# Gate and up of the last token block as seven products of halves, with the sums of weights formed one block earlier

## Chip, core and metric

One core of one Trainium2 chip runs the whole kernel. The metric is the device time of one execution in microseconds (us). The core has five engines, each of which works through its own list of instructions in order: TensorE (PE; its weight loads are shown apart as PEld), VectorE (DVE), ScalarE (ACT), GpSimd (POOL) and SyncE (SP), which issues nearly all transfers. The transfers themselves run on 16 DMA engines.

## The reference

One layer of a sequence model with 2048 tokens, D = 1024, everything in float32. Four mixers (S5, HGRN2, FoX attention, mLSTM) work on projections of the normed input; their outputs are joined, projected by `w_out`, and a gated feed-forward follows, each with a norm before and after:

```python
        mix = jnp.concatenate([y_a, y_b, y_c, y_d], axis=-1) @ w_out[l]
        h = h + rms_norm(mix, ln_mix_post[l])
        a = rms_norm(h, ln_ffn_pre[l])
        ff = (jax.nn.silu(a @ w_ffn_gate[l]) * (a @ w_ffn_up[l])) @ w_ffn_down[l]
        h = h + rms_norm(ff, ln_ffn_post[l])
```

The change concerns `a @ w_ffn_gate` and `a @ w_ffn_up`; both weights are 1024 x 2816.

## The kernel before, in words

**Numbers.** TensorE multiplies in a format (fp32r) that holds only the upper part of a float32. So each operand is split into two such parts, hi and lo, and each product is three matmuls: hi by hi, lo by hi, hi by lo. In the names, a weight's parts are wh and wl (dh and dl for the down weights), an activation's b_ah and b_al.

**Blocks.** The 2048 tokens are worked in four blocks of 512 (b = 0 to 3), a block being four row tiles of 128. The mixers of block b + 1 are laid beside the feed-forward of block b; the last block's feed-forward has nothing beside it. For each block `Attn.proj` first multiplies by `w_out`, and then, for each row tile t, takes a square sum, forms 1/rms on GpSimd (L1415, L1416), loads the row of x (b_xt, L1419), adds it, stores the sum for later (h_d, L1421), takes a second norm (rsqrt_mean, L67 and L68 on GpSimd), and hands the normed row to `transpose_parts`: eight 128 x 128 transposes on TensorE (L102), in two groups of four, each of which is copied as hi by ACT (L104) and subtracted as lo by DVE (L105). b_xt has two buffers (pool `x`).

**Feed-forward.** The 2816 columns are 22 tiles f of 128. For each f, `gate_up` loads the gate and up weights (four tiles of 128 x 1024, 512 KB each) and runs 48 matmuls (L1469): gate and up, times eight pieces of D, times three parts, each with 512 token columns. The first two f run in two cuts of 256 columns, so that the first cut needs only row tiles 0 and 1. Then tanh (ACT, L1473), two DVE operations, a hi copy and a lo subtraction give g_h. For two f at a time `down` multiplies by the down weights (eight loads of 256 KB; 48 matmuls, L1494) and adds into b_acc on DVE (L1499).

**Weights.** `split_load` reads a weight in the first block into a raw tile (wr), forms hi on ACT (L87) and lo on GpSimd (L88), and stores both parts to DRAM; from the second block on it reloads the two parts with two SP loads (L83). The rings wh, wl, dh and dl have four buffers each, wr has two. A load waits on SP until its buffer's last reader is done, and what is behind it in SP's list waits too.

**Order.** The program's text names the work, and a scheduler that ran when the kernel was built put it in an order on each engine. The engines then run that fixed order.

The functions that the change touches, and what calls them:

## Time and profile before

| | before |
|---|---|
| median of 3 runs | 2805.01 us (2796.91 to 2816.34) |
| the profiled execution, its own time | 2805.62 us |
| its span on the core | 2803.9 us |
| PE, matmuls | 2692.5 us, 96% of the span |
| PEld, weight loads | 2270.0 us, 81% |
| DVE | 1541.4 us, 55% |
| POOL | 837.9 us, 30% |
| ACT | 778.3 us, 28% |
| moved by DMA | 605.04 MB, mean 216 GB/s |

The busy time of an engine is the time in which at least one of its instructions is running. PE's matmuls overlap each other, so its busy time is no sum of single durations, and the price of one more matmul is read from start to start. PEclk is the share of full TensorE clock granted in a stretch; a DMA share of 1 means that all 16 DMA engines were moving all the time. The gap of 1.7 us between span and time lies outside of the traced instructions.

### The profile page before, as it was taken

How to read it: one execution, taken by the hardware profiler on the slowest of the kernel's cores; microseconds unless marked ns; L12 is line 12 of the kernel's file. 1: busy time of each engine (PE TensorE's matmuls, PEld its weight loads, DVE VectorE, ACT ScalarE, POOL GpSimd, SP SyncE). 2: the span in 40 equal slices, each digit the busy share in tenths (PEclk: the TensorE clock that was granted, in tenths of full speed). 3: DMA queues.
4: the chain of work that ended last, by engine and by line, in shares of the span. 5: the costliest groups of instructions: out<-in, count | busy, mean ns of one | idle time of the engine just before them, and what ended most of it. 6: DMA issues, size and time to landing. Idle time of an engine off the chain costs nothing.

```text
span 2803.9 us, 39055 instructions
## 1 busy us (share of the span) xinstructions
PE 2692.5 (96%) x14294; PEld 2270.0 (81%) x14294; DVE 1541.4 (55%) x2522; ACT 778.3 (28%) x1502; POOL 837.9 (30%) x927
## 2 busy tenths in 40 slices
PE   6898999999999999999899999999999999999998
PEld 5787987988888778787787788888878788888886
DVE  7958466483225665865466656545666554322333
ACT  5322336233223333324221232222122331200001
POOL 7554311243125567542111234211022330100001
PEclk9899999999999999999999999999999999999999
DMA  6573696535778878696756566575656656755553
GB/s 228 195 261 123 207 293 209 169 122 210 241 230 292 287 258 282 201 310 232 255 172 214 198 195 206 177 285 187 215 181 194 202 182 230 285 195 186 193 195 135
DMA packets 323103, 605.04 MB, mean 216 GB/s; under 512 B 56160, under 2 KB 146144, under 8 KB 322656
## 3 DMA queue, kind: packets, MB, share of 16 engines
q1 hardware_dynamic: 321888, 602.48, 64.2%
q8 instruction: 113, 1.85, 0.3%
q14 instruction: 78, 0.64, 0.1%
q0 software_dynamic: 1024, 0.07, 0.0%
HBM read 428.42 MB, written 173.35 MB: 215 GB/s over the span
## 4 chain that ended last, share of the span: by engine, by line
PE 73%; DVE 9%; DMA 8%; issue 3%; POOL 2%; SPq 2%; ACT 2%; POOLq 0%; DVEq 0%; ACTq 0%
PE pf L1469 29%; PE pf L1494 15%; PE pf L1386 6%; PE pf L288 5%; PE pf L270 5%; PE ps L903 2%; DVE hQ L511 2%; PE ps L887 1%; PE ps L886 1%; PE ps L828 1%; DVE hA L525 1%; DMA b_xt<-in_x_dram 1%; PE pt L102 1%; PE ps L521 1%; DMA wh<-wu1h 1%
## 5 line engine op out<-in xcount | busy, mean ns | idle before, releaser
L1469 PE MATMUL pf<-b_ah,wh 128*128 128x512 f32 (+1 forms) x1536 | 580.5, 378 | 4.4 <-ACT b_ah L104 4.4
L1469 PE MATMUL pf<-b_ah,wl 128*128 128x512 f32 (+1 forms) x1536 | 579.8, 378 | 0.0
L1469 PE MATMUL pf<-b_al,wh 128*128 128x512 f32 (+1 forms) x1536 | 578.2, 378 | 0.0
L1494 PE MATMUL pf<-dh,g_h 128*128 128x512 f32 x1408 | 461.3, 396 | 1.8 <-DVE b_acc L1499 1.5
L1469 PEld LDWEIGHTS pf<-b_ah,wh 128*128 128x128 f32 x1536 | 291.3, 190 | 60.4 <-ACT b_ah L104 5.3
L1469 PEld LDWEIGHTS pf<-b_ah,wl 128*128 128x128 f32 x1536 | 291.3, 190 | 55.0
L1469 PEld LDWEIGHTS pf<-b_al,wh 128*128 128x128 f32 x1536 | 289.5, 189 | 54.4
L1494 PEld LDWEIGHTS pf<-dh,g_h 128*128 128x128 f32 x1408 | 264.8, 189 | 58.7 <-DVE b_acc L1499 3.4
L1494 PE MATMUL pf<-dl,g_h 128*128 128x512 f32 x704 | 277.5, 394 | 0.0
L1499 DVE TENSOR_TENSOR b_acc<-b_acc,pf 128x512 f32<-128x512 f32 x320 | 215.7, 684 | 105.9 <-PE pf L1494 103.5
L900 POOL TENSOR_TENSOR f_accs<-f_accs,f_pe 128x512 f32<-128x512 f32 (+3 forms) x144 | 172.7, 1199 | 293.6 <-ACT f_pe L894 290.7
L88 POOL TENSOR_TENSOR wl<-wr,wh 128x1024 fp32r<-128x1024 f32 (+2 forms) x76 | 185.6, 2444 | 208.6 <-ACT wh L87 137.3
L896 DVE TENSOR_TENSOR f_pl<-f_pe,f_ph 128x512 fp32r<-128x512 f32 (+3 forms) x160 | 184.6, 1162 | 88.9 <-ACT f_ph L895 75.7
L288 PE MATMUL pf<-wl,aTh 128*128 128x256 f32 (+2 forms) x768 | 220.7, 287 | 0.2 <-DMA wl<-wi_1l 0.2
L288 PE MATMUL pf<-wh,aTh 128*128 128x256 f32 (+2 forms) x768 | 220.7, 288 | 0.0
L288 PE MATMUL pf<-wh,aTl 128*128 128x256 f32 (+2 forms) x768 | 220.2, 287 | 0.0
L1473 ACT ACTIVATE g_th<-pf 128x512 f32<-128x512 f32 x88 | 52.5, 597 | 412.2 <-PE pf L1469 412.1
L1474 DVE SCALAR_TENSOR_TENSOR g_th<-g_th,pf 128x512 f32<-128x512 f32 x88 | 60.3, 685 | 191.8 <-ACT g_th L1473 191.5
L270 PE MATMUL pf<-aTh,wh 128*128 128x512 f32 (+1 forms) x400 | 158.9, 398 | 2.7 <-ACT aTh L104 2.7
L270 PE MATMUL pf<-aTh,wl 128*128 128x512 f32 (+1 forms) x400 | 157.7, 395 | 0.0
L270 PE MATMUL pf<-aTl,wh 128*128 128x512 f32 (+1 forms) x400 | 156.9, 394 | 0.1
L1475 DVE TENSOR_TENSOR g_th<-g_th,pf 128x512 f32<-128x512 f32 x88 | 60.2, 684 | 174.8 <-PE pf L1469 174.7
(510 smaller groups left out, 4812.7 us busy)
## 6 DMA issues: line engine op xcount, KB each, us to landing
dh<-wd_0h SPq DMA_DIRECT2D x66, 256.0 KB
dl<-wd_0l SPq DMA_DIRECT2D x66, 256.0 KB
dh<-wd_1h SPq DMA_DIRECT2D x66, 256.0 KB
dl<-wd_1l SPq DMA_DIRECT2D x66, 256.0 KB
wr<-in_w_ffn_gate_dram SPq DMA_DIRECT2D x22, 512.0 KB
wr<-in_w_ffn_up_dram SPq DMA_DIRECT2D x22, 512.0 KB
dr<-in_w_ffn_down_dram SPq DMA_DIRECT2D x44, 256.0 KB
f_KB<-kb_d SPq DMA_DIRECT2D x80, 132.0 KB
```

The lines of the kernel that those rows point to most:

```text
L88: nc.gpsimd.tensor_tensor(lo, r, f32(hi), ALU.subtract)
L270: nc.tensor.matmul(l3(pt)[:, cut], lhsT=x[k][:, s], rhs=a[:, cut, k], start=(n == 0), stop=(n == 23))
L288: nc.tensor.matmul(pt[:, :w], lhsT=a[:, t, k], rhs=x[k], start=(n == 0), stop=(n == 23))
L511: nc.vector.tensor_tensor(Q[s, hh].rearrange("p (n w) -> p n w", w=h), q3[s, :, h - 1:2 * h - 1], eq[s], ALU.mult)
L896: nc.vector.tensor_tensor(pl[:, cs], pe[:, cs], f32(ph[:, cs]), ALU.subtract)
L900: nc.gpsimd.tensor_tensor(accs[:, cs], accs[:, cs], pe[:, cs], ALU.add)
L1386: nc.tensor.matmul(pt, lhsT=a[:, t, k], rhs=w, start=(first and i == 0), stop=(last and i == 2))
L1469: nc.tensor.matmul(l3(pt)[:, s], lhsT=x[:, k], rhs=a[:, s, k], start=(k == 0 and i == 0), stop=(k == KD - 1 and i == 2))
L1474: nc.vector.scalar_tensor_tensor(th, th, 1.0, pts[0], ALU.add, ALU.mult)
L1475: nc.vector.tensor_tensor(th, th, pts[1], ALU.mult)
L1494: nc.tensor.matmul(pt, lhsT=a[:, s], rhs=w[:, 0], start=(m == 0), stop=(m == 3 * len(fs) - 1))
L1499: nc.vector.tensor_tensor(acc[:, t, ns], acc[:, t, ns], pt, ALU.add)
```

## The change

In the **last block** gate and up are no longer 22 times two products of 512 tokens with D = 1024. Two tiles f and f + 1 form a pair q (11 pairs), and for a pair the tokens are halved (row tiles 0, 1 and row tiles 2, 3), D is halved, and the columns are halved (f and f + 1). The eight products of halves become seven (the scheme of Strassen in Winograd's form), between sums of halves. Each of the seven is 24 matmuls of 256 columns: gate and up, four pieces of D, three parts.

- Activations: `Halves.put` forms the sums of rows T1 to T4 and transposes seven operands of 256 tokens and 512 of D into g_U, 56 transposes in all where there were 32. b_xt of row tiles 2 and 3 takes a buffer of wr.
- Weights: products 0, 2 and 5 use the stored hi and lo parts as they are, in four loads of 256 KB each. Products 1, 3, 4 and 6 use sums of weights: one load of 512 KB in full float32, then hi on ACT and lo on DVE (1 and 4) or GpSimd (3 and 6).
- Results: partial sums lie in a tile C, and DVE makes seven adds of 512 columns for each pair out of PSUM.
- Order: products 0 and 2 of the first two pairs come first (`head`); they need row tiles 0 and 1 alone.

In the **third block** (b = 2) `Halves.keep` forms the sums of weights: for each pair, for gate and for up, SP loads four quarters (256 KB each, in pieces of 512 B), GpSimd makes four sums in place, and GpSimd's own queue stores them to DRAM. The four tiles (ws_0 to ws_3) have one buffer each. This makes 22 groups of four loads, four sums and four stores.

The diff, cut to its core:

```diff
-    for h in range(0, KD, 4):
+    for h in range(0, x.shape[1] // P, 4):
...
+class Halves:
+    def __init__(self, c):
+        self.c = c
+        self.w = [x[0].rearrange("(k p) n -> p k n", p=P) for x in (c.w_ffn_gate, c.w_ffn_up)]
+        self.kept = {(q, i): c.dram.tile([P, D], F32, name=f"ws{q}_{i}") for q in range(c.w_ffn_gate.shape[2] // (2 * P))
+                     for i in (1, 3, 4, 6)}
+    def keep(self, pool, q, m):
+        nc = self.c.nc
+        tiles = [pool.tile([P, 512], F32, name=f"ws_{n}", tag=f"ws_{n}") for n in range(4)]
+        for r, k, f in zip(tiles, (0, 0, 4, 4), (0, 1, 1, 0)):
+            n0 = (2 * q + f) * P
+            nc.sync.dma_start(r.rearrange("p (k n) -> p k n", k=4), self.w[m][:, k:k + 4, n0:n0 + P])
+        X11, X21, X22, X12 = tiles
+        for i, s, x, y, op in ((3, X11, X11, X21, ALU.subtract), (4, X21, X21, X22, ALU.add),
+                               (1, X22, X22, X11, ALU.subtract), (6, X12, X12, X22, ALU.subtract)):
+            nc.gpsimd.tensor_tensor(s, x, y, op)
+        for i, s in ((3, X11), (4, X21), (1, X22), (6, X12)):
+            nc.gpsimd.dma_start(self.kept[q, i][:, m * 512:m * 512 + 512], s)
+    def load(self, q, i):
+        c, nc = self.c, self.c.nc
+        hi, lo = (c.pw.tile([P, WRING], F32R, name=n, tag=n)[:, 0:D] for n in ("wh", "wl"))
+        if i in (0, 2, 5):
+            k0, f = {0: (0, 0), 2: (512, 0), 5: (512, 1)}[i]
+            for t, part in ((hi, 0), (lo, 1)):
+                for m, n in enumerate("gu"):
+                    nc.sync.dma_start(f32(t[:, m * 512:m * 512 + 512]),
+                                      c.parts[f"w{n}{2 * q + f}"][part][:, k0:k0 + 512])
+            return hi, lo
+        nc.sync.dma_start(f32(lo), self.kept[q, i])
+        nc.scalar.activation(hi, f32(lo), AF.Copy)
+        (nc.vector if i in (1, 4) else nc.gpsimd).tensor_tensor(lo, f32(lo), f32(hi), ALU.subtract)
+        return hi, lo
+    def operand(self, i, t):
+        u = self.U[:, 2 * i + t].rearrange("p (d k t) -> p d k t", d=2, k=4)
+        return u[:, 0], u[:, 1]
+    def put(self, t, xs, rows):
+        c, nc = self.c, self.c.nc
+        a, b = slice(0, 512), slice(512, D)
+        if t < 2:
+            new = ((0, xs[t][:, a]), (2, xs[t][:, b]))
+        else:
+            x, x1 = xs[t - 2], xs[t]
+            s1, s2 = rows(), rows()
+            T1, T2, T3, T4 = s1[:, a], s1[:, b], s2[:, a], s2[:, b]
+            nc.vector.tensor_tensor(T1, x1[:, a], x[:, a], ALU.subtract)
+            nc.vector.tensor_tensor(T2, x1[:, b], T1, ALU.subtract)
+            nc.gpsimd.tensor_tensor(T3, x1[:, b], x1[:, a], ALU.subtract)
+            nc.vector.tensor_tensor(T4, x[:, b], T2, ALU.subtract)
+            new = ((1, T2), (3, T3), (4, T1), (5, T4), (6, x1[:, b]))
+        for i, v in new:
+            transpose_parts(c, c.psS, "s", v, *self.operand(i, t % 2))
...
-    def proj(self, b):
+    def proj(self, b, halves=None):
...
-            xt = self.xtile("b_xt")
+            if halves is None or t < 2:
+                xt = self.xtile("b_xt")
+            else:
+                xt = c.pwr.tile([P, WRING], F32, name="b_xt2", tag="wr")[:, 0:D]
...
-            transpose_parts(c, c.psS, "s", xt, ah[:, t], al[:, t])
+            if halves is None:
+                transpose_parts(c, c.psS, "s", xt, ah[:, t], al[:, t])
+            else:
+                xs.append(xt)
+                halves.put(t, xs, self.row)
...
-    def run(b, hook):
+    def run(b, hook, step, halves):
...
+        def gate_up_halves():
+            C = attn.p.tile([P, 4, D], F32, name="g_c", tag="b_al").rearrange("p t n -> p (t n)")
+            C = C.rearrange("p (b q j m t) -> p b q j m t", b=2, q=2, j=2, m=2)
+            def product(q, i):
+                wh, wl = halves.load(q, i)
+                pt = ptile()
+                pv = pt.rearrange("p (m j t) -> p m j t", m=2, j=2)
+                for m in range(2):
+                    for k in range(4):
+                        for n, (w, d) in enumerate(((wh, 0), (wl, 0), (wh, 1))):
+                            k0 = (4 * m + k) * P
+                            nc.tensor.matmul(pv[:, m], lhsT=w[:, k0:k0 + P],
+                                             rhs=halves.U[:, 2 * i:2 * i + 2, d * 512 + k * P:d * 512 + (k + 1) * P],
+                                             start=(k == n == 0), stop=(k == 3 and n == 2))
+                return pt.rearrange("p (m t) -> p m t", m=2)
+            def add(dst, pt, x):
+                nc.vector.tensor_tensor(dst, pt, x, ALU.add)
+            def gated(f, v):
+                th, h = p2.tile([P, BLK], F32, name="g_th", tag="th"), h_tile()
+                t, h4 = (x.rearrange("p (j t) -> p j t", t=256) for x in (th, h))
+                nc.scalar.activation(t, v[:, :, 0], AF.Tanh, scale=0.5)
+                nc.vector.scalar_tensor_tensor(t, t, 1.0, v[:, :, 0], ALU.add, ALU.mult)
+                nc.vector.tensor_tensor(t, t, v[:, :, 1], ALU.mult)
+                nc.scalar.activation(h4[:, 0:2], t, AF.Copy, scale=0.5)
+                nc.vector.scalar_tensor_tensor(h4[:, 2:4], t, 0.5, f32(h4[:, 0:2]), ALU.mult, ALU.subtract)
+                pend.append((f, h[:, 0:BLK], h[:, BLK:]))
+            def head(q):
+                c1 = C[:, q % 2, 0]
+                nc.scalar.activation(c1[:, 1], product(q, 0), AF.Copy)
+                add(c1[:, 0], product(q, 2), c1[:, 1])
+            def tail(q):
+                c1, c2 = C[:, q % 2, 0], C[:, q % 2, 1]
+                add(c1[:, 1], product(q, 1), c1[:, 1])
+                add(c2[:, 0], product(q, 3), c1[:, 1])
+                pt = product(q, 4)
+                add(c1[:, 1], pt, c1[:, 1])
+                add(c2[:, 1], pt, c2[:, 0])
+                add(c1[:, 1], product(q, 6), c1[:, 1])
+                gated(2 * q, c1)
+                add(c2[:, 0], product(q, 5), c2[:, 0])
+                gated(2 * q + 1, c2)
+            for q in range(NF // 2):
+                if q == 0:
+                    head(0)
+                    head(1)
+                elif q > 1:
+                    head(q)
+                tail(q)
+                if q:
+                    down(pend[:2], q == 1)
+                    del pend[:2]
...
-        gate_up((0, 1), (slice(0, 2), slice(2, 4)))
-        for f in range(2, NF):
+        if halves is not None:
+            gate_up_halves()
+        else:
+            gate_up((0, 1), (slice(0, 2), slice(2, 4)))
+        for f in range(2, NF if halves is None else 0):
+            if f % 2 == 0:
+                step(f // 2 - 1)
             gate_up((f,), (slice(0, 4),))
             if len(pend) == 3 and f < NF - 1:
                 down(pend[:2], pend[0][0] == 0)
                 pend = pend[2:]
+        step(NF // 2 - 1)
...
+        halves = Halves(c)
+        sums = None
+
+        def step(b, q):
+            if b == NB - 2:
+                for m in range(2):
+                    halves.keep(sums, q, m)
+
         for b in range(NB):
+            last = b == NB - 1
+            if last:
+                stack.close()
+                pool = s.enter_context(tc.tile_pool(name="g_u", bufs=1, side="left", reuse_waits="tile"))
+                halves.U = pool.tile([P, 14, D], F32R, name="g_U")
             if b:
-                attn.proj(b)
+                attn.proj(b, halves if last else None)
+            if b == NB - 2:
+                stack = ExitStack()
+                sums = stack.enter_context(tc.tile_pool(name="w_sums", bufs=1, side="left", reuse_waits="tile"))
             if b + 1 < NB:
                 mixers(b + 1)
-            ffn(b, lambda: attn.pre(b + 1) if b + 1 < NB else None)
+            ffn(b, lambda: attn.pre(b + 1) if b + 1 < NB else None, lambda q: step(b, q), halves if last else None)
```

**Where the instructions stand.** First SP's list at the start of the third block's feed-forward. b_xt is the row of x, h_d the stored row, wg1h the hi part of the gate weights of tile 1, ws_ a tile of the sums. Before:

```order
L1419 DMA b_xt<-in_x_dram 128x1024
L1421 DMA h_d_224<-b_acc 128x1024 x2
L1419 DMA b_xt<-in_x_dram 128x1024
L83 DMA wh<-wg1h 128x1024
L83 DMA wl<-wg1l 128x1024
L83 DMA wh<-wu1h 128x1024
L83 DMA wl<-wu1l 128x1024
L83 DMA dh<-wd_0h 128x512
```

and in the changed kernel:

```order
L1490 DMA b_xt<-in_x_dram 128x1024 x2
L1354 DMA ws_20926<-in_w_ffn_gate_dram 128x4x128
L1354 DMA ws_20927<-in_w_ffn_gate_dram 128x4x128
L1354 DMA ws_20928<-in_w_ffn_gate_dram 128x4x128
L1354 DMA ws_20929<-in_w_ffn_gate_dram 128x4x128
L1492 DMA h_d_224<-b_acc 128x1024 x2
L83 DMA wh<-wg1h 128x1024
L83 DMA wl<-wg1l 128x1024
L83 DMA wh<-wu1h 128x1024
L83 DMA wl<-wu1l 128x1024
L83 DMA dh<-wd_0h 128x512
```

A whole group of four sum loads now stands between the loads of b_xt and the stores of the rows, ahead of the weights of tile 1.

Second, GpSimd's list at the same place, where it forms the 1/rms of the row tiles (L1415, L1416, L67 and L68 before; L1483, L1484, L67 and L68 after). Before:

```order
L1404 TENSOR_SCALAR b_ss<-b_ss 128x4
L1415 TENSOR_SCALAR b_rs<-b_ss 128x1
L1416 TENSOR_TENSOR b_rs<-b_rs,mhalf 128x1
L67 TENSOR_SCALAR b_rs<-b_rs 128x1
L68 TENSOR_TENSOR b_rs<-b_rs,mhalf 128x1
L1415 TENSOR_SCALAR b_rs<-b_ss 128x1
```

and in the changed kernel, in the second row tile:

```order
L1484 TENSOR_TENSOR b_rs<-b_rs,mhalf 128x1
L1358 TENSOR_TENSOR ws_20926<-ws_20926,ws_20927 128x512
L1358 TENSOR_TENSOR ws_20927<-ws_20927,ws_20928 128x512
L1360 DMA ws_3_8752<-ws_20926 128x512
L1358 TENSOR_TENSOR ws_20928<-ws_20928,ws_20926 128x512
L1360 DMA ws_4_8753<-ws_20927 128x512
L67 TENSOR_SCALAR b_rs<-b_rs 128x1
L1483 TENSOR_SCALAR b_rs<-b_ss 128x1
L1358 TENSOR_TENSOR ws_20929<-ws_20929,ws_20928 128x512
L1360 DMA ws_1_8751<-ws_20928 128x512
L68 TENSOR_TENSOR b_rs<-b_rs,mhalf 128x1
```

The sums and their stores now stand between the steps of one row tile's 1/rms.

Third, SP's list in the middle of the last block. ws_1_8763 is a stored sum (product 1 of a pair), wg11h a stored hi part. Before:

```order
L83 DMA dl<-wd_0l 128x512
L83 DMA dh<-wd_0h 128x512 x2
L83 DMA dl<-wd_0l 128x512
L83 DMA dl<-wd_1l 128x512
L83 DMA dh<-wd_1h 128x512 x2
L83 DMA dl<-wd_1l 128x512
L83 DMA wl<-wg17l 128x1024
L83 DMA wh<-wg17h 128x1024
```

and in the changed kernel:

```order
L1373 DMA wl<-ws_1_8763 128x1024
L1373 DMA wl<-ws_3_8764 128x1024
L83 DMA dl<-wd_0l 128x512
L83 DMA dh<-wd_0h 128x512 x2
L83 DMA dl<-wd_0l 128x512
L83 DMA dl<-wd_1l 128x512
L83 DMA dh<-wd_1h 128x512 x2
L83 DMA dl<-wd_1l 128x512
L1373 DMA wl<-ws_4_8765 128x1024
L1373 DMA wl<-ws_6_8766 128x1024
L1370 DMA wl<-wg11l 128x512
L1370 DMA wh<-wg11h 128x512
```

The down weights stand where they stood, between groups of gate and up loads; the loads of products 1 and 3 stand ahead of them and those of 4, 6 and 5 behind.

## Rows read from the trace of the kernel before

**Rows 1.** The page's first part: engine, busy us, share, instructions.

```profile
PE 2692.5 (96%) x14294; PEld 2270.0 (81%) x14294; DVE 1541.4 (55%) x2522; ACT 778.3 (28%) x1502; POOL 837.9 (30%) x927
```

**Rows 2.** Stretches: us; busy PE, PEld, DVE, ACT, POOL (instructions); PEclk, DMA share, GB/s.

```profile
1800.00:2200.00 400.00, 395.89 (x1923) 323.91 (x1922) 222.68 (x338) 94.65 (x187) 75.41 (x92) 1.00 0.65 217
...
1900.00:1910.00 10.00, 8.71 (x65) 7.96 (x64) 4.39 (x5) 3.21 (x8) 2.60 (x4) 1.00 1.01 375
...
2441.00:2780.00 339.00, 339.00 (x1504) 277.56 (x1504) 98.28 (x144) 26.45 (x43) 0.00 (x0) 1.00 0.56 186
```

**Rows 3.** PE's waits, 2400 to 2804: who for whom, sum us, times, longest.

```profile
PE pf L1469 <- ACT b_ah L104: 1.7, 2, 1.4
PE pt L102 <- DVE b_xt L1425: 1.4, 1, 1.4
```

**Rows 4.** The chain in order of time: start us, us, what.

```profile
269.03 20.14 PE pf L288 x169
...
1905.58 9.06 DMA b_xt<-in_x_dram
...
2422.73 7.89 DMA b_xt<-in_x_dram
```

**Rows 5.** Stretches, line L1469 alone: PE busy, PEld busy, PEclk, DMA share, GB/s.

```profile
2437.00:2448.00 11.00, 11.00 (x97) 11.00 (x98) 1.00 0.55 187
...
2422.00:2434.00 12.00, 11.37 (x96) 11.19 (x96) 1.00 1.02 378
...
2448.00:2780.00 332.00, 224.61 (x962) 180.21 (x960) 1.00 0.55 184
```

**Rows 6.** Timeline of PE at the last block's start: us, us of one, what, count.

```profile
2426.13 1.03 PE L102 MATMUL pt<-ident,b_xt 128*128 128x128 f32 x8
2426.92 0.37 PE L1469 MATMUL pf<-b_al,wh 128*128 128x256 f32 x1
```

**Rows 7.** Groups by line and shape: count; busy us, mean ns; idle before, releasers.

```profile
L88 POOL TENSOR_TENSOR wl<-wr,wh 128x1024 fp32r<-128x1024 f32 x72 | 174.9, 2430 | 201.6 <-ACT wh L87 130.3 <-DMA ka_d<-flo 53.8 <-DMA dr<-in_w_ffn_down_dram 8.0
...
L900 POOL TENSOR_TENSOR f_accs<-f_accs,f_pe 128x512 f32<-128x512 f32 x96 | 134.3, 1399 | 213.4 <-ACT f_pe L894 211.7
...
L87 ACT ACTIVATE wh<-wr 128x1024 fp32r<-128x1024 f32 x72 | 76.0, 1055 | 85.2 <-PE pf L1469 24.8 <-DMA wr<-in_w_ffn_gate_dram 19.1 <-PE pf L270 12.0
...
L105 DVE TENSOR_TENSOR b_al<-pt,b_ah 128x512 fp32r<-128x512 f32 x64 | 41.6, 685 | 44.2 <-ACT b_ah L104 43.9
...
L1530 DVE TENSOR_TENSOR b_acc<-b_acc,g_h 128x1024 f32<-128x1024 f32 x12 | 14.8, 1229 | 7.6 <-DMA g_h<-in_ln_ffn_post_dram 4.8 <-ACT junk L1332 2.6
```

**Rows 8.** Timeline of SP in the last block: us, us, DMA issue.

```profile
2575.11 0.32 SPq L83 DMA_DIRECT2D wl<-wg11l  x1
2575.53 0.38 SPq L83 DMA_DIRECT2D wh<-wg11h  x1
```

**Rows 9.** DMA traffic from 2570 to 2580 in 40 slices of 0.25 us.

```profile
GB/s 41 180 377 393 418 401 328 279 295 262 319 377 221 139 90 16 0 0 0 0 0 0 0 0 131 147 147 262 262 377 311 426 377 442 426 377 377 131 0 0
```

**Rows 10.** Timeline of SP around and in the third block's feed-forward.

```profile
1800.66 0.56 SPq L83 DMA_DIRECT2D dl<-wd_1l  x1
...
2056.68 0.33 SPq L83 DMA_DIRECT2D wl<-wg9l  x1
...
2102.80 0.32 SPq L83 DMA_DIRECT2D wl<-wg11l  x1
...
2190.21 0.32 SPq L83 DMA_DIRECT2D wl<-wg15l  x1
```

**Rows 11.** GpSimd's own transfers: ns of an issue (min, median, max), when; landing.

```profile
L872 POOL DMA_DIRECT2D f_QB<-f_mr x32: 497/520/814, 461.5 to 2192.8; - x32
...
DMA to landing us min/median/max: 1.6/3.5/5.6
```

1 line of the change is left out of this document (added).

## The prediction

> **What bounds the kernel now.** I read the page first, then the stretches of the two blocks that the change touches, then what TensorE waits for there, then the chain. The page's first part says that TensorE has a matmul in flight for 96% of the span [rows 1]. The stretches say it more sharply: over the last block's feed-forward (2441 to 2780 us) PE is busy in all 339 us, at full clock (PEclk 1.00, which is the 2.4 GHz level), with DVE at 98, ACT at 26 and GpSimd at 0 us, and the DMA engines at a share of 0.56 [rows 2]. PE waits there for nothing but 1.7 and 1.4 us at the block's start [rows 3]. So a matmul column taken away in this block is time taken away, as long as nothing new makes PE wait. In the third block (1800 to 2200 us) PE is busy for 395.9 of 400 us, the DMA engines have a share of 0.65 and move 217 GB/s, and GpSimd works 75 us; but in its start, 1900 to 1910, the DMA share is already 1.01 at 375 GB/s and PE is idle for 1.3 of 10 us [rows 2]. There the chain runs through a transfer: the load of b_xt takes 9.06 us of it, as the like load in the last block takes 7.89 [rows 4]. So the last block has room on every engine but PE, and the third block has room on GpSimd, little on the DMA engines, and none at its start.
>
> **The products (last block).** Before: 22 tiles f, of which two run in two cuts of 256 columns (192 matmuls) and 20 run as 48 matmuls of 512 (960). After: 11 pairs times 7 products times 24 matmuls of 256 columns = 1848. PE's matmuls overlap, so their price is from start to start. 962 of 512 columns take 224.61 us: 0.2335 each. 97 of 256 columns take 11.00 us: 0.1134 each with a DMA share of 0.55; 96 take 11.37 us, 0.1184 each, with a share of 1.02 [rows 5]. The longest unbroken run of 256-column matmuls, of another line, is 169 in 20.14 us, 0.1192 each [rows 4]. Halving the columns costs almost nothing, then: the 128-column weight load before each stays hidden. The new block moves, for each pair, 5 MiB of gate and up weights (three products of 1 MiB, four of 0.5) and 2 MiB of down weights, where 6 MiB moved before; a pair takes about 30 us, so 7.34 MB in 30.3 us is 242 GB/s, against 186 now, a DMA share of 0.56 x 242/186 = 0.73. Between the two prices at 0.55 and 1.02 that gives 0.1153. Before: 960 x 0.2335 + 192 x 0.1134 = 245.9 us. After: 1848 x 0.1153 = 213.1. **Saved: 32.8 us**; bounds 36.3 (at 0.1134) and 25.7 (at 0.1192).
>
> The Trainium skill (TensorE: Matmul & The Clock Gate, section "Wait — 56ns, not 53.3ns?") has start-to-start at the columns divided by 2.4 GHz plus about 2.5 ns, which is 109.2 ns for 256 columns and 215.8 ns for 512. By that page's figures the saving would be an estimated 228.1 - 201.8 = 26.3 us, not 32.8. The trace does not agree: its 512-column matmuls of this line cost 0.2335, more than two of 256 (0.1134 each), so the rows decide.
>
> **The operands.** The 32 transposes of the block become 56. Eight take 0.79 us from start to start [rows 6], so 24 more are 2.4 us of PE: **+2.4 us**. Each four of them need an ACT copy and a DVE subtraction of 0.69 us [rows 7], and the last two row tiles need three more DVE operations and one on GpSimd. They are covered by the four products (0 and 2 of the first two pairs, 96 matmuls, 11 us) that need only the first two row tiles. Those tiles' b_xt no longer wait for a buffer of two, so they can start earlier than the 7.89 us transfer lets them now; the 3.1 us of waiting may go or may grow by as much. Taken as 0; ends -3 and +5.
>
> **The ring of four (last block).** A product's weights go into a ring of four, so a load starts when the product four before it ends and must be ready three products, 3 x 24 x 0.1153 = 8.3 us, later. Two loads of 512 KB issued at 2575.1 and 2575.5 [rows 8] move their bytes between 2576.0 and 2579.5 (40 slices of 0.25 us) [rows 9]: 4.4 us for 1 MB, an estimated 3.5 for one. Then the ACT copy (1.06) and the subtraction, 1.23 on DVE (products 1 and 4) or 2.43 on GpSimd (3 and 6) [rows 7]: 3.5 + 1.06 + 2.43 = 7.0 us. It fits with 1.3 us to spare, and for half of the products 11 us of down matmuls lie between as well. DVE's work for a pair, 7 adds, 6 gating operations, 8 down adds and 2 subtractions, is 21 x 0.69 + 2.5 = 17 us of 30. I take **+2 us**; ends 0 and 13 (below).
>
> **The sums (third block).** 22 groups of four 256 KB loads by SP, four GpSimd sums and four stores by GpSimd's own queue: 23.1 MB read and 23.1 MB written. In SP's order the first load stands behind a down weight load that SP issued at 1800.66, and the last before the load of gate tile 15, issued at 2190.21 [rows 10]. That is 389.6 us, 17.7 us for a group and 118 GB/s on top of 217, 335 in all; the full stretch moved 375. So on average they fit, with a duty near 0.9. GpSimd's part is 88 sums of 1.40 [rows 7] and 88 issues, for which the nearest row is 0.52 us for a small DMA [rows 11]: 169 us on top of the 75 it does in 400. It has the time.
>
> At the block's start they do not fit. Around the b_xt loads SP now issues a group (1 MB), with about as many stores in flight, where the share was 1.01: 2.1 MB at 375 GB/s are 5.6 us by which b_xt, and the weights of tile 1, come later, on the chain. GpSimd puts two sums and their stores between the two halves of a row tile's 1/rms as well (the order rows). **+6 us**; ends 0 (the groups' loads wait themselves) and 12.
>
> The Trainium skill (DMA: Bandwidth & Descriptors, section "Issuing engines are not separate DMA queues") says that a queue of another engine runs on the same 16 DMA engines and saves issue time alone. It speaks against expecting anything of GpSimd's own queue; this trace agrees only so far that the share reaches 1.01 with nearly all bytes on one queue, and nothing in it shows two queues with much to move. Had the stores engines of their own, the start would cost 2.8 us, not 5.6.
>
> In the rest of the block SP's weight loads run well ahead: tile 9's are issued at 2056.68, and its buffer is freed, for tile 11's, at 2102.80 [rows 10]; its gate product takes 24 x 0.2335 = 5.6 us, so it begins near 2097. That is 40 us ahead, 36 after a landing of 4.4. This hides the slips of single groups. **+2 us**; ends 0 and 54 (below).
>
> **Sum:** -32.8 + 2.4 + 0 + 2 + 6 + 2 = -20.4 us. The profiled execution took 2805.62 us, 0.6 over the median of the three runs: 2785.2, forecast **2785 us**.
>
> **The rivals.** *Everything added is hidden*: the products and transposes alone, -30.4, up to -33.9 with the lowest price: 2772 to 2775. For it: the bursts of [rows 9] leave the DMA engines idle between; against it: 1.01 at the third block's start.
>
> *The ring is too short.* If a landing in the last block takes 6 us, as loads on the chain do where much is queued (7.89 and 9.06 for this size [rows 4]), product 6 is ready after 9.5 us, 1.2 late in each of 11 pairs: +13 instead of +2, 2796 us; at 7 us it is +24, 2807. For it: the eight down loads stand right ahead of product 4's in SP's order. Against it: the DMA share is 0.73 there.
>
> *Slower: SP stands still before a slot.* The four tiles of a group have one buffer each. A load of the next group waits on SP until the store from its tile has landed, and behind it wait all weight loads. Chain of a slot: landing, two sums, two issues, landing: 4.4 + 2.8 + 1.0 + 4.4 = 12.6 us, under the 17.7 that SP's order gives it. With both landings at the 9.06 us of the full stretch [rows 4] it is 21.9: each of 22 groups slips 4.2 us, 92 in all, less the 36 that the ring hides: +56 instead of +2, **2839 us**. It costs nothing below a period of 17.7 + 36/22 = 19.3 us, and eats the gain at 20.3. For it: 335 GB/s on average for 390 us. Against it: the bursts reach 375 and more, and 9 us is a landing at full share.
>
> **How the numbers follow.** Forecast (2777 to 2796) 0.53; all hidden (2772 to 2777) 0.20; ring (2796 to 2807) 0.12; SP (2800 to 2840) 0.15, of which 0.09 above 2833. Measurement of this kernel can tell about 1%, 28 us: faster by over that is below 2777, so 0.20; slower above 2833, so 0.09; within, 0.71. The range 2772 to 2812 leaves out 0.05 below and some 0.13 above.
>
> **What would show it.** The last block's line of products should have 1848 matmuls at 0.113 to 0.119 us start to start, and 2441 to the end some 30 us shorter. A ring that is too short shows as PE waiting for ACT or GpSimd on wh or wl, once per pair. The third block's start should show PE's wait for b_xt grown by some 6 us, and a DMA share near 0.9 until about 2190. The slower rival shows as SP waiting for GpSimd's stores for more than 4 us per group and PE waiting for DMA on weights. I am wrong if PE's idle time in the third block grows by over 20 us, or if the products cost above 0.125 us.

## The result and the profile after

The changed kernel takes 2824.27 us (median of 7 runs, 2818.59 to 2832.87), the kernel before 2805.01 (7 runs). The ratio is 1.0072, with a 95% interval of 1.0051 to 1.0094: 19 us slower, where 20 us faster was forecast, and outside the range of 2772 to 2812.

The profiled execution has a span of 2831.1 us, 27.2 over before's. Below it is cut at the first matmul of a block's `w_out` product (stages) and at PE's last matmul (end):

| us | up to third block | third block | last block | end | span |
|---|---|---|---|---|---|
| before | 1857.4 | 517.0 | 417.0 | 12.5 | 2803.9 |
| after | 1866.3 | 542.3 | 405.3 | 17.2 | 2831.1 |
| difference | +8.9 | +25.3 | -11.7 | +4.7 | +27.2 |

The first column is scatter: in kernels that differ only from the third block on it lies between 1848.8 and 1866.3. Without it 18.3 us are left, near the 19.3 between the medians. So the last block gained two fifths of what was forecast (11.7 of 28.4 us), the third block lost three times as much (25.3 for 8), and the end, which the sum did not have, lost too.

The page's first part after, which answers [rows 1]:

```profile
PE 2684.2 (95%) x15014; PEld 2295.6 (81%) x15014; DVE 1666.4 (59%) x2633; ACT 835.0 (29%) x1563; POOL 1064.5 (38%) x1127
```

Stretches after, with the columns of [rows 2]: two at the third block's start, one in its middle, two in the last block:

```profile
1866.00:1906.00 40.00, 35.38 (x142) 28.30 (x141) 17.39 (x15) 5.75 (x14) 20.94 (x24) 0.91 1.00 358
1906.00:1946.00 40.00, 31.06 (x189) 27.51 (x188) 18.32 (x19) 11.13 (x22) 23.66 (x31) 0.89 0.84 295
2006.00:2186.00 180.00, 174.42 (x769) 138.84 (x768) 110.92 (x160) 32.82 (x61) 99.77 (x108) 0.99 0.94 307
2450.00:2500.00 50.00, 46.67 (x349) 44.13 (x349) 36.08 (x44) 21.69 (x33) 17.39 (x14) 0.97 0.82 284
2600.00:2800.00 200.00, 199.91 (x1375) 186.14 (x1375) 113.65 (x152) 45.97 (x58) 29.69 (x12) 1.00 0.68 223
```

The same first two stretches of the kernel before:

```profile
1857.00:1897.00 40.00, 40.00 (x175) 32.57 (x174) 18.45 (x20) 8.73 (x20) 7.23 (x14) 1.00 0.79 297
1897.00:1937.00 40.00, 35.98 (x269) 33.02 (x268) 22.73 (x33) 13.27 (x28) 9.63 (x17) 0.96 0.65 237
```

In the first 80 us of the third block the DMA share is 1.00 and 0.84 where it was 0.79 and 0.65, PE runs 331 matmuls instead of 444, and its granted clock is 0.91 and 0.89. This is a mean: most of the time it is at 2.4 GHz, but at 1.2 GHz from 1892.5 to 1899.3, 1923.2 to 1926.7 and 1940.3 to 1947.1, stretches that begin in or right behind the three gaps of PE there. In the whole third block 20.5 us are at 1.2 GHz, where it was 3.4. In the middle the share is 0.94 and PE is idle 5.6 us of 180. In the last block PE has no gap over 0.3 us from 2551 to 2802; between 2600 and 2800 it is busy 199.91 of 200 us.

What PE waited for longest from 1790 to the end (sum us, times, longest), which answers [rows 3]; and what SP waited for longest from 1780 to 2420 (SPq is SP's list):

```profile
PE pt L102 <- DVE b_xt L1496: 8.7, 2, 6.6
PE ps L828 <- DMA f_KB<-kb_d: 4.8, 3, 2.5
PE pf L1453 <- ACT junk L1332: 4.6, 1, 4.6
```

```profile
SPq L1354 <- DMA ws<-ws: 117.2, 48, 7.1
```

The first and third of PE's waits lie at the block's start, the second in its middle: f_KB is a load for FoX attention, which runs beside the feed-forward. SP stood 117 us before tiles of the sums whose store had not landed. One such case: SP stands from 2120.7 to 2127.4, the f_KB loads behind it in its list are issued at 2132.1 and 2135.3, and PE stands for f_KB from 2137.5 to 2140.0. The loads of the sums (ns of an issue, then first and last start), and the landing of their stores:

```profile
L1354 SPq DMA_DIRECT2D ws<-in_w_ffn_gate_dram x44: 367/384/2875, 1809.5 to 2201.6; - x44
L1354 SPq DMA_DIRECT2D ws<-in_w_ffn_up_dram x44: 368/384/459, 1832.8 to 2217.8; - x44
```

```profile
DMA to landing us min/median/max: 2.4/5.2/7.3
```

22 groups from 1809.5 to 2217.8, 408.3 us, are 18.6 us each.

### The profile page after: what moved, and what is told of

Its sections match the earlier page's. It is cut to its first block, busy times and chain, and to the rows that moved or that the text cites. A ratio compares the mean times of both kernels' runs of the same rounds, so it can differ in the third digit from the quotient of the medians.

```text
span 2831.1 us, 41412 instructions
## 1 busy us (share of the span) xinstructions
PE 2684.2 (95%) x15014; PEld 2295.6 (81%) x15014; DVE 1666.4 (59%) x2633; ACT 835.0 (29%) x1563; POOL 1064.5 (38%) x1127
## 5 line engine op out<-in xcount | busy, mean ns | idle before, releaser
L1544 PE MATMUL pf<-b_ah,wh 128*128 128x512 f32 (+1 forms) x1152 | 438.4, 381 | 1.7 <-ACT b_ah L104 1.7
L1544 PE MATMUL pf<-b_ah,wl 128*128 128x512 f32 (+1 forms) x1152 | 437.8, 380 | 0.0
L1544 PE MATMUL pf<-b_al,wh 128*128 128x512 f32 (+1 forms) x1152 | 434.9, 379 | 0.0
L1544 PEld LDWEIGHTS pf<-b_ah,wh 128*128 128x128 f32 x1152 | 219.8, 191 | 43.1 <-ACT b_ah L104 2.2
L1544 PEld LDWEIGHTS pf<-b_ah,wl 128*128 128x128 f32 x1152 | 219.8, 191 | 41.1
L1544 PEld LDWEIGHTS pf<-b_al,wh 128*128 128x128 f32 x1152 | 218.1, 190 | 40.8
L1569 PE MATMUL pf<-g_U,wh 128*128 128x256 f32 x1232 | 224.5, 284 | 2.2 <-ACT wh L1374 1.1
L1569 PEld LDWEIGHTS pf<-g_U,wh 128*128 128x128 f32 x1232 | 191.9, 191 | 3.6 <-ACT wh L1374 1.5
L1569 PE MATMUL pf<-g_U,wl 128*128 128x256 f32 x616 | 173.0, 284 | 1.0 <-POOL wl L1375 0.9
L1358 POOL TENSOR_TENSOR ws<-ws,ws 128x512 f32<-128x512 f32 x88 | 119.0, 1352 | 137.3 <-DMA ws<-in_w_ffn_up_dram 60.3
```

The source lines that it names most:

```text
L1358: nc.gpsimd.tensor_tensor(s, x, y, op)
L1544: nc.tensor.matmul(l3(pt)[:, s], lhsT=x[:, k], rhs=a[:, s, k], start=(k == 0 and i == 0), stop=(k == KD - 1 and i == 2))
L1569: nc.tensor.matmul(pv[:, m], lhsT=w[:, k0:k0 + P], rhs=halves.U[:, 2 * i:2 * i + 2, d * 512 + k * P:d * 512 + (k + 1) * P], start=(k == n ...
```

## Experiments

Ratios are to runs of the kernel before on the same chip and use all runs, so they are not the quotient of the two medians; the last three columns are lengths in the profiled execution, as in the table above. e14 and e15 have one run each.

| run | median us (before) | ratio, 95% | third block | last block | end |
|---|---|---|---|---|---|
| e1, no sums | 2792.9 (2804.5) | 0.9949, 0.9931 to 0.9968 | 517.4 | 402.5 | 11.4 |
| e2, sums only | 2830.7 (2804.5) | 1.0093, 1.0069 to 1.0116 | 540.3 | 416.8 | 18.0 |
| e3, loads only | 2816.8 (2804.5) | 1.0041, 1.0028 to 1.0054 | 531.1 | 417.8 | 12.1 |
| e4, stores by SP | 2823.2 (2804.5) | 1.0066, 1.0045 to 1.0088 | 550.3 | 406.0 | 11.4 |
| e5, held back | 2820.1 (2804.0) | 1.0054, 1.0037 to 1.0071 | 541.7 | 405.4 | 17.2 |
| e6, no stores | 2825.1 (2804.0) | 1.0069, 1.0049 to 1.0088 | 541.2 | 416.9 | 12.2 |
| e7, cuts of 256 | 2804.6 (2804.0) | 0.9999, 0.9984 to 1.0013 | 517.3 | 413.9 | 12.5 |
| e8, two blocks | 2854.3 (2804.0) | 1.0170, 1.0154 to 1.0185 | 517.6 | 404.8 | 17.3 |
| e9, two blocks, held | 2801.7 (2802.6) | 0.9995, 0.9983 to 1.0007 | 515.9 | 407.1 | 17.2 |
| e10, the same, stores by SP | 2793.8 (2802.6) | 0.9975, 0.9960 to 0.9989 | 517.8 | 404.0 | 11.7 |
| e11, held, loads by GpSimd | 2826.3 (2802.6) | 1.0082, 1.0054 to 1.0109 | 521.3 | 436.3 | 11.4 |
| e12, last block on DVE | 2788.9 (2802.6) | 0.9951, 0.9936 to 0.9967 | 519.1 | 398.5 | 11.4 |
| e13, e10 and DVE | 2795.6 (2803.0) | 0.9966, 0.9952 to 0.9981 | 516.9 | 402.2 | 12.5 |
| e14, groups of 12 | 2803.6 (2803.0) | one run | 517.2 | 413.8 | 12.5 |
| e15, tokens from b_ah | 2788.7 (2803.0) | one run | 518.1 | 395.2 | 10.6 |
| e16, e13 with g_U moved | 2785.1 (2803.4) | 0.9944, 0.9925 to 0.9963 | 517.2 | 395.2 | 10.8 |

### The halves apart: e1 and e2

e1:

```diff
+            return
-            if b == NB - 2:
-                for m in range(2):
-                    halves.keep(sums, q, m)
...
-        nc.sync.dma_start(f32(lo), self.kept[q, i])
+        nc.sync.dma_start(f32(lo), c.parts[f"w{'gu'[i % 2]}{2 * q + i // 4}"][0])
```

> The changed kernel without the sums of weights in the third block; in the last block products 1, 3, 4 and 6 load a stored hi part of the same size (512 KB) in place of the sum, so the numbers are wrong but every load, copy, subtraction, matmul and add of the last block is there. Theory (the loss is in the third block, the last block gains less than forecast): the third block is as before, the last block some 12 to 17 us shorter than before, 2788 to 2796 us. Rival (the last block's own gain is eaten elsewhere too, by a later end of the kernel): 2800 to 2810. If GpSimd's queue with many bytes is what makes the kernel end 5 us later after its last store, that 5 us is gone here.

e2:

```diff
-                attn.proj(b, halves if last else None)
+                attn.proj(b, None)
...
-            ffn(b, lambda: attn.pre(b + 1) if b + 1 < NB else None, lambda q: step(b, q), halves if last else None)
+            ffn(b, lambda: attn.pre(b + 1) if b + 1 < NB else None, lambda q: step(b, q), None)
```

> The kernel before with only the sums added in the third block (22 groups of loads, GpSimd sums and stores by GpSimd's queue); nothing reads them, the last block is as before. Theory: 20 to 33 us slower than before (2825 to 2838), of which about half is PE idle at the third block's start and behind late FoX loads and the rest matmuls at a lower granted clock. Rival (the third block's loss comes from the last block's operand buffers taking room or order): below 10 us slower.

By the medians the seven products alone gain 11.5 us, and the sums alone cost 26.2. Both theories held; the rivals (the gain eaten after the last block, the loss made by the operand buffers) fell. The end is 11.4 us without the sums and 18.0 with them.

### Which part of the sums: e3, e6 and e4

e3 leaves out the GpSimd sums and the stores, e6 the stores alone; both have the last block of before. e4 is the changed kernel with

```diff
-            nc.gpsimd.dma_start(self.kept[q, i][:, m * 512:m * 512 + 512], s)
+            nc.sync.dma_start(self.kept[q, i][:, m * 512:m * 512 + 512], s)
```

> As the run with the sums only, but the 88 loads alone: no GpSimd sums and no stores, so half of the added bytes and no tile that waits for a store. Theory (DMA engines are what is short): 8 to 15 us slower than before, PE idle at the third block's start still 4 us or more above before. Rival (GpSimd's own list and its stores are the cause): within 4 us of before. Rival (SP standing before a tile whose store has not landed is the cause): within 4 us too, and no wait of SP for a store is left.

> As the run with the sums only, but the 88 stores left out: loads and GpSimd sums alone. Theory (bytes at the block's start, and SP standing before stores in its middle): between the run with loads only (+12 us) and the run with sums and stores (+26): +10 to +18, no PE wait for FoX loads in the block's middle, and the end of the kernel after PE's last matmul back from 18 to 12 us. Rival (GpSimd's sums cost the time): still +20 or more.

> The changed kernel with the 88 stores issued by SP in place of GpSimd. Theory (the bytes matter, not the queue): within 8 us of the changed kernel, third block's start as slow. Rival (GpSimd's queue, its 0.56 us issues and its end of kernel cost the time): 10 us or more faster than the changed kernel, and the 7 us without any work at the end of the kernel back to 2. Rival (SP's own stall): slower than the changed kernel, since a store then also holds SP until its sum is done.

Loads alone cost 12.4 us, all at the block's start, where nothing held them back and they ran one after the other. e3, its first 140 us of the block, and PE's longest wait in it:

```profile
1855.80:1995.80 140.00, 125.68 (x694) 106.76 (x693) 68.36 (x111) 33.13 (x72) 26.28 (x41) 0.94 1.02 333
```

```profile
PE pf L1448 <- ACT junk L1332: 11.1, 1, 11.1
```

With the GpSimd sums (e6) it is 21.1. That is past the +10 to +18 expected, and past the +20 at which the rival, that the GpSimd sums cost the time, was to hold: they add 8.7 us to the loads, and all but 0.7 of PE's 19.8 us of idle in the block lies before 1950. How they make the start longer was not taken apart. With the stores (e2) it is 26.2. The stores do not lengthen the third block (540.3 against 541.2) but move its loss: PE idles 12.3 us at the start and 6.3 behind it, for 19.1 and 0.7 without them. And they add 5.8 us to the end.

With SP's queue in place of GpSimd's (e4) the end is back at 11.4, and the third block is 8 us longer, so that the time is as before the edit (2823.2 for 2824.3). SP then stands 65 us before stores that wait for a sum and 42 before tiles, not more in all than the 117 of the changed kernel; of PE's 14.8 us of idle in the block's middle 8.1 are for FoX's loads and 6.4 for a gating result of DVE. Nothing here shows that a second queue gave bandwidth. The Trainium skill (DMA: Bandwidth & Descriptors, section "Issuing engines are not separate DMA queues") says that transfers run on the same 16 DMA engines whichever engine issued them; e4's time agrees with it, but is no clean test, since the edit also made SP stand for sums.

### Where the sums lie: e5, e8, e9, e10, e11

e5 lets GpSimd first copy a column of a late result into the four tiles, and the loads wait for it:

```diff
+        if token is not None:
+            for r in tiles:
+                nc.gpsimd.tensor_copy(r[:, 0:1], token)
...
+                for p in ((), (0,), (1,), (2,), (3,), (4,), (5,), (6,), (7,), (8,), (9, 10))[q]:
+                    for m in range(2):
+                        halves.keep(sums, p, m, f32(pend[-1][1])[:, 0:1] if p == m == 0 else None)
```

> The changed kernel with the sums held back: none before tile 4 of the third block's feed-forward (GpSimd copies a column of a result of that time into the four tiles, and the loads wait for it); two groups per pair of tiles from there, four in the last step. Theory (over half of the third block's loss is made at its start, on the path of b_xt, the rows and the w_out weights): the start is as before (PE idle there 4 us, granted clock no lower), some 12 to 17 us faster than the changed kernel, 2807 to 2812. Rival (the loss is per byte, wherever the sums lie): within 4 us of the changed kernel, with more PE idle in the block's middle and end.

The start was as before (PE idle 4.4 us there), and still the block took 541.7: the loss moved into the middle, where PE idles 16.2 us. The theory that most of the loss belongs to the start fell. From here on two readings stood: every group costs its bytes, or SP's standing costs.

e8 gives gate's sums to the second block and up's to the third, without holding them:

```diff
-            if b == NB - 2:
-                for m in range(2):
-                    halves.keep(sums, q, m)
+            if NB - 3 <= b <= NB - 2:
+                halves.keep(sums, q, b - NB + 3)
...
```

> The changed kernel with the sums over two blocks: those of gate in the second block, those of up in the third, half the rate in each, same bytes in all. Theory (what costs is the DMA engines near full at the starts and SP's waits before stores, which vanish below a share of 0.8): 5 to 15 us faster than the changed kernel, 2809 to 2819, no slot wait of SP over 3 us in the blocks' middle. Rival (cost per byte): within 4 us of the changed kernel.

It did not spread them. The scheduler took all 22 groups into the second block as fast as the tiles came free, which its loads show:

```profile
L1354 SPq DMA_DIRECT2D ws<-in_w_ffn_gate_dram x44: 367/383/1047, 1322.0 to 1527.5; - x44
L1354 SPq DMA_DIRECT2D ws<-in_w_ffn_up_dram x44: 368/384/823, 1533.3 to 1729.6; - x44
```

The second block took 587.7 us, where the kernels without sums in it take 528 to 537, and the third 517.6. The run says nothing on half the rate, but it says that the same groups cost 50 us or more where they cover the second block's start at full rate. e9 holds each group by its own copy, gate in the second block and up in the third:

```diff
+            if NB - 3 <= b <= NB - 2:
+                for p in ((), (0,), (1, 2), (3,), (4, 5), (6,), (7,), (8,), (9,), (10,), ())[q]:
+                    halves.keep(sums, p, b - NB + 3, f32(pend[-1][1])[:, 0:1])
...
```

> The changed kernel with the sums of gate in the second block and those of up in the third, each group held back by a GpSimd copy of a column of a result of its time, so that none runs ahead: none at a block's start, one group of four per 18 to 36 us instead of one per 18.6. Theory (the sums cost through two places only: the block's start, and SP standing before a tile whose store has not landed; the bytes themselves lie beside PE's work): no PE idle above before's in either block, 22 fewer slot waits over 3 us, only the last block's gain (-11.5 us, measured without the sums) and the longer end of the kernel (+5.6) stay: 2796 to 2803. Rival (each group costs its bytes wherever it lies, about 1 us): within 5 us of the run with the sums held back in one block, 2815 to 2825.

e10 is e9 with the stores on SP:

> As the run with the sums over two blocks, held back, with the 88 stores issued by SP instead of GpSimd. Theory: the 5.6 us at the end of the kernel are gone, at most 3 us of new waits behind stores that wait for a sum: 2791 to 2799, faster than before by 0.2 to 0.5%. Rival (SP's waits for GpSimd's sums cost as much as the end gains): as the run with GpSimd's stores.

e11 is e5 with the loads on GpSimd's queue, so that SP never stands before them:

```diff
-            nc.sync.dma_start(r.rearrange("p (k n) -> p k n", k=4), self.w[m][:, k:k + 4, n0:n0 + P])
+            nc.gpsimd.dma_start(r.rearrange("p (k n) -> p k n", k=4), self.w[m][:, k:k + 4, n0:n0 + P])
```

> The run with the sums held back in the third block, with their 88 loads issued by GpSimd's queue too, so that SP never stands before a tile of the sums. Same bytes, same 330 us. Theory (SP's standing is what made 16 us of PE idle in the block's middle): PE's waits for FoX loads (f_KB, f_QA, f_V, b_y) go from 16 us to under 5, and the time to 2803 to 2812, unless GpSimd, which now waits itself, is late with FoX's sums: then PE waits for DVE or POOL results instead. Rival (DMA engines near 0.9 make those loads late): PE idle for DMA stays at 10 us or more, time within 4 us of 2820.

The same 360 us of the third block in e5, e9 and e11, in this order, and SP's waits for stores in e5 (1780 to 2400) and e9 (1320 to 2400):

```profile
1994.00:2354.00 360.00, 346.94 (x1533) 275.37 (x1532) 204.67 (x274) 86.19 (x168) 242.49 (x252) 0.99 0.90 299
```

```profile
1990.00:2350.00 360.00, 359.90 (x1619) 287.72 (x1618) 217.12 (x298) 89.56 (x171) 183.12 (x216) 1.00 0.80 258
```

```profile
1994.00:2354.00 360.00, 356.29 (x1594) 284.56 (x1594) 234.83 (x286) 86.89 (x170) 266.32 (x286) 1.00 0.88 287
```

```profile
SPq L1357 <- DMA ws<-ws: 144.4, 57, 7.5
```

```profile
SPq L1357 <- DMA ws<-ws: 10.4, 4, 3.5
SPq L1357 <- POOL ws L1354: 37.2, 27, 8.2
```

(The second line of e9 is SP's wait for the holding copies.) e9 has half of the groups in this stretch, 11, and PE loses 0.1 us; at 1 us a group it would lose 11, so "per byte" fell. Its second block takes 536.3 us, at the upper end of what kernels without sums there show. The four kernels with held sums there take 535.7 to 537.1, 536.5 on average, and the thirteen without 532.1: held groups still cost some 4 us in that block. e9 holds each group and halves the rate at once; which of the two did more, no run tells.

e11 has a share of 0.88, near e5's 0.90, and PE idles 3.7 us instead of 13.1. None of it is for a load; in e5 6.1 us are for loads and 6.9 for results of DVE. So it is SP's standing that makes FoX's loads late, not the share. But e11 as a whole failed: GpSimd, which now stood itself, ran late, its last store went out at 2449.2, in the last block, and PE waited there:

```profile
L1363 POOL DMA_DIRECT2D ws<-ws x88: 540/570/626, 1998.4 to 2449.2; - x88
```

```profile
PE pf L1456 <- ACT junk L1332: 14.5, 1, 14.5
```

That stage took 436.3 us, 31 more than e5's. e10 came out at 2793.8, as its theory had it. In the like stretch (1986 to 2346) SP stands there for sums instead:

```profile
SPq L1363 <- POOL ws L1361: 39.9, 36, 2.5
```

PE loses 0.3 us of these 360. So SP's standing as such is not what costs. Its longest single stands before loads or stores of the sums are 7.1 and 7.5 us in the changed kernel and e5, and 3.3 and 2.5 in e9 and e10 in this stretch; that their length decides is argued from this, not tested, and in e4 stands of at most 4.6 us went with 8.1 us of PE waiting for FoX's loads.

### The last block: e7, e12 to e16

e7 is the kernel before with all its tiles of the last block in two cuts:

```diff
-            gate_up((f,), (slice(0, 4),))
+            gate_up((f,), (slice(0, 2), slice(2, 4)) if last else (slice(0, 4),))
```

> The kernel before, with gate and up of all 22 tiles of the last block in two cuts of 256 columns (1920 matmuls more of 256, 960 fewer of 512), the same loads. It measures the price of a 256-column matmul in a long stretch with the DMA traffic of before (share 0.56). Theory A (0.1193 us, as the products of the changed kernel took, is the price of any long stretch): 1920 x 0.1193 - 960 x 0.2335 = +5 us, 2810. Theory B (0.1146 to 0.1153, as in the short second cut of before; the products are slower for their own traffic or operands): -3 to -4 us, 2801.

Its median did not move (0.9999), its last block is 3.1 us shorter. e14 adds a new accumulation group every 12 matmuls to that (`start` and `stop` at every fourth k), which leaves half of the sum over D out of its result:

> The kernel before with the last block in two cuts of 256 columns, and in it accumulation groups of 12 matmuls instead of 24 (the result then holds only the second half of the sum over D, so its numbers are wrong). It asks why a product's matmul takes 0.1191 us where one of the cuts takes 0.1144: a product has groups of 12. Theory (the change of group costs): 0.119 here. Rival (operands or their place): still 0.1144.

e12 is e1 with all subtractions on DVE and hi and lo of g_U in two tiles:

```diff
-        (nc.vector if i in (1, 4) else nc.gpsimd).tensor_tensor(lo, f32(lo), f32(hi), ALU.subtract)
+        nc.vector.tensor_tensor(lo, f32(lo), f32(hi), ALU.subtract)
...
```

> The changed kernel without the sums (products 1, 3, 4 and 6 load a stored part of the same size; numbers wrong for that reason), with two edits in the last block: all 44 subtractions on DVE, none on GpSimd, and hi and lo of the operands in two tiles instead of one. Theory 1: DVE's gating operations of 1.04 and 1.21 us on average take 0.69 and below 0.9 without GpSimd beside them, and PE's 3.5 us of waits for b_acc go: 2 to 4 us faster than the run without sums, 2789 to 2791. Theory 2: the products' 0.1191 us goes to 0.1144 if the layout of the operands made them slower: then 9 us more, 2780 to 2783. Rivals: no change of the price, and DVE's longer list eats what it gains.

e15 is e1 with another operand:

```diff
-    rhs=halves.U[:, 2 * i:2 * i + 2, d * 512 + k * P:d * 512 + (k + 1) * P],
+    rhs=attn.ah[:, 2 * (i % 2):2 * (i % 2) + 2, 4 * d + k],
```

> The changed kernel without the sums, in which the matmuls of the products read their tokens from the tile b_ah, as the kernel before does, instead of from g_U (numbers wrong for that reason). Theory (the place of g_U in memory makes a matmul slower): 0.1144 here. Rival (the products' loop or what runs beside it): 0.119.

e13 is e10 with the subtractions on DVE; e16 is e13 with the pool of g_U opened with `side="right"`, the end of the on-chip memory at which b_ah lies, instead of `side="left"`:

> The run with the sums over two blocks, held back and stored by SP, with all 44 subtractions of the last block on DVE. If the two gains add (-8.7 us for the first against before, -4.0 for the second against the run without sums): 2788 to 2793, 0.3 to 0.5% faster than before. Rival (they overlap): 2794 as without the second edit.

> The run with the sums over two blocks, held back and stored by SP, and all subtractions on DVE, with one edit more: the memory of g_U is taken from the other end of the on-chip memory, next to b_ah, from which a matmul of this shape takes 0.115 us (0.1193 from g_U's old place). Theory (the place alone sets the price): 0.114 to 0.116, 8 us faster than that run, 2786 to 2789. Rival (b_ah is faster for another reason than its end of the memory): still 0.119, 2793 to 2797.

From the chain of the last block in the changed kernel, in e7, e14, e13 and e16, in this order (start us, us, what, count), and two matmuls of e15:

```profile
2467.70 9.54 DMA wl<-ws
...
2553.25 20.07 PE pf L1569 x168
...
2584.26 20.01 PE pf L1569 x168
```

```profile
2474.02 21.97 PE pf L1469 x192
```

```profile
2471.15 21.97 PE pf L1469 x192
```

```profile
2580.55 20.04 PE pf L1572 x168
```

```profile
2513.44 19.26 PE pf L1572 x168
2543.79 19.15 PE pf L1572 x168
```

```profile
2638.73 0.28 PE L1569 MATMUL pf<-b_ah,wh 128*128 128x256 f32 x1
...
2657.99 0.28 PE L1569 MATMUL pf<-b_ah,wh 128*128 128x256 f32 x1
```

A matmul of a product takes 20.04 / 168 = 0.1193 us. The cut of 256 columns takes 21.97 / 192 = 0.1144 over a whole block, with groups of 24 as of 12: it is neither the length of the stretch nor the group. e12's two tiles left it at 0.1193. In e15 seven products in a row start their first and last matmul at 2638.73 and 2657.99, so 19.26 / 167 = 0.1153; other such stretches of it have 0.1135 and 0.1146. And in e16, whose source moves g_U and changes nothing else, it is 19.2 / 168 = 0.1143. The place of the tokens in memory makes 5 ns per matmul (most start 113 or 114 ns apart in e16, 120 in e13), and 7.0 us of the last block (402.2 to 395.2); why is open. e16 is 18.3 us faster than before, the fastest version here that does the whole work, and 1 us beyond its expected range. e13 missed its range of 2788 to 2793: at 2795.6 the gain of the moved subtractions doesn't show in its time.

DVE's gating, the two operations that read th and the sums C, in the changed kernel and in e12:

```profile
L1582 DVE TENSOR_TENSOR g_th<-g_th,g_c 128x512 f32<-128x512 f32 x22 | 26.7, 1214 | 0.4
L1581 DVE SCALAR_TENSOR_TENSOR g_th<-g_th,g_c 128x512 f32<-128x512 f32 x22 | 22.9, 1039 | 8.3 <-ACT g_th L1580 8.3
```

```profile
L1580 DVE SCALAR_TENSOR_TENSOR g_th<-g_th,g_c 128x512 f32<-128x512 f32 x22 | 15.1, 688 | 7.6 <-ACT g_th L1579 7.6
L1581 DVE TENSOR_TENSOR g_th<-g_th,g_c 128x512 f32<-128x512 f32 x22 | 15.1, 687 | 0.3
```

Both read two operands from on-chip memory (SBUF) now, where one came from PSUM before. In the changed kernel they take 1.04 and 1.21 us on average, in e12 0.69. The average is of two kinds: 33 of the 44 take 0.69 there too, and 11 take 2.3 to 2.7. Each of the 11 starts while a GpSimd subtraction (L1375) runs, and ends some 0.55 us after it; five that started before one kept to 0.69. The Trainium skill (SBUF — State Buffer, section "Who interferes with whom") says that a DVE instruction with two SBUF inputs contends with a GpSimd instruction that reads SBUF; the trace agrees with these 11. On the path it is worth 2 to 4 us of the stage (402.5 to 398.5 in e12, which also has two tiles, and 404.0 to 402.2 in e13); the times can't tell it (e1 0.9949 against e12 0.9951).

## Why the prediction was wrong

Two steps failed. The products were priced by DMA share, from rows that read another operand; and the sums were held to cost nothing in the middle of the third block, since the weights of the feed-forward run ahead, with no look at the loads that do not. The largest miss in us is the third block, 25.3 for 8.

**The products** (-32.8): 1848 x 0.1193 - 245.9 = -25.4, just under the lower bound given (25.7). The price of 0.1153 came from two stretches that read b_ah, 0.1134 at a DMA share of 0.55 and 0.1184 at 1.02 [rows 5]. But from start to start most matmuls of both are 0.113 or 0.114 us apart; the two prices differ by gaps in the second stretch, and by matmuls that the ends of the first cut through. And the row of the other line, 0.1192 [rows 4], which served only as a bound, comes from a stretch with a low share:

```profile
269.03:289.17 20.14, 20.14 (x172) 20.09 (x171) 4.86 (x8) 7.24 (x14) 6.81 (x6) 1.00 0.54 158
```

So the rows of before already spoke against a price by share. That 0.1192 lies at the measured 0.1193 may be chance: no run tells whether it has the same cause. e7, e14 and e16 show that neither the length of the stretch, the group nor the products' own traffic (a share of 0.70 in e16 as in e13, 2443 to 2760) sets the price, and that the operand's place does. With g_U moved the term is 1848 x 0.1143 - 245.9 = -34.7. The Trainium skill (TensorE: Matmul & The Clock Gate, section "Wait — 56ns, not 53.3ns?") led to an estimate of 26.3, which lies near the measured 25.4. This is luck: its 109.2 and 215.8 ns are each below what was measured, 114 to 119 and some 230 ns.

**Transposes, operands, ring** (+4.4): the rest of the last block is -11.7 + 25.4 = +13.7. PE idles 8.5 us instead of 3.2, 7.2 of it before 2551, while the first sums land (9.54 us) and DVE's gating is slow; the granted clock falls a little there (0.97). The slow gating was not priced at all. Counted from start to start without the gaps, the products gain 21.2 us (245.4 to 224.2, at the block's start dearer than 0.1193), the transposes cost 2.1 as forecast, the other matmuls 2.1 more, and 5.3 are PE's longer idle time: -11.7. The ring of four was right: 0.1 us of idle in 200.

**The third block's start** (+6): PE's idle there grew from 4.0 to 13.3 us, +9.3, of the foreseen kind and within its bounds. What was missing is the price of idling: the same matmuls of the block keep PE busy for 521.2 us instead of 513.0, +8.2, at a granted clock of 0.91 and 0.89 in the first two stretches instead of 1.00 and 0.96. It fits the time at 1.2 GHz: half of 20.5 - 3.4 us is 8.5.

**The chain of the sums** (+2): +7.5 us of idle in the middle, 4.8 of it straight for f_KB. This is the step that failed by its reasoning. The period of 18.6 us was nearly foreseen (17.7), and the rule was that nothing is lost below 19.3, since SP's weight loads run 36 us ahead. The weights were indeed never late in the middle. But SP has one list, and FoX's loads in it have no such lead: with SP standing up to 7.1 us, they reached PE late. What stands behind a waiting instruction has to be named load by load, not for the loads with the longest lead. e9 and e11 show it from both sides. The slower rival thus had SP's standing right, and the loads that it delays and the threshold wrong. The measured time lies in that rival's range (2800 to 2840), but by another sum: its +56 us measured +7.5.

**The end** (none): +4.7 us in this profile; with GpSimd's stores 17.2 to 18.0 in five kernels and 11.4 in a sixth (e11), without them 10.6 to 12.5.

The sum: -20.4, + 7.4 products, + 9.3 rest of the last block, + 17.3 third block (25.3 in place of 8), + 4.7 end = +18.3 us, the measured 19. Every term that missed did so to the same side. Neither sign of being wrong that was named came: PE's idle time in the third block grew by 17.1 us, not by over 20, and the products cost 0.1193, not above 0.125. The time came out wrong without either of them.

## What to carry to other kernels

Work that is put beside a full engine must also fit the queue that issues it: a load that waits for its tile's store holds every load behind it, and those with the least lead decide. Hold such work back from stretches where the DMA engines are already full, give each piece a dependency on a result of its time (a scheduler runs what is merely free ahead of time, e8), and leave the pieces room; here, with the stores on SP, that turned the sums' +26 us into some 3 (e10's -8.7 against the -11.5 of e1, medians that are not clear of each other). A matmul's price is best taken from start to start, without gaps, and from a row that reads its operand from the same place.

## What was not expected of the hardware

- The same matmul of 256 columns takes 0.1193 or 0.1143 us depending on where in the on-chip memory its tokens lie (e13 and e16).
- In five of the six kernels with GpSimd's stores, which had long landed, the end is 5 to 6 us longer: after the last store of the output has moved its bytes nothing moves for 8 us (changed kernel, 40 slices of 0.5 us from 2812), and for 3 us in e10 (from 2771, with one small packet more):

```profile
GB/s 0 0 0 0 0 16 0 352 385 373 385 78 287 238 90 381 385 193 0 0 283 385 369 12 0 0 0 0 0 0 0 0 0 0 0 0 0 0 0 0
```

```profile
GB/s 0 0 0 0 0 0 0 0 0 0 0 0 0 0 0 0 0 70 365 385 385 365 25 373 131 176 385 385 103 0 4 369 373 303 0 0 0 0 16 0
```

What runs in that time is GpSimd's closing DRAIN (the longest of three; ns min/median/max); all engines go on 0.2 us after its end. In the changed kernel and in e11:

```profile
L1853 POOLq DRAIN  x3: 46/93/10498, 2819.9 to 2830.9; - x3
```

```profile
L1857 POOLq DRAIN  x3: 46/93/1927, 2823.4 to 2828.6; - x3
```

It takes 10.5 to 11.5 us in the five and 1.9 to 4.3 in all others; in the changed kernel SP's own ends 5.8 us before it. The bytes of the queue alone don't make it long: e11 has the loads on that queue too. What it waits for is open.
